# Attention scores from a stacked key and a 64-row product of the query's low part

## The chip, the cores and the metric

The kernel runs on one core of a Trainium2 chip. The metric is the device time of one execution in microseconds (us): less is better. TensorE (PE in the profile) multiplies matrices, VectorE (DVE), ScalarE (ACT) and GpSimd (POOL) work elementwise, and SyncE's queue (SP) issues the transfers. A matrix product on TensorE is two records: the load of the stationary operand (LDWEIGHTS, engine PEld) and the product proper (MATMUL, engine PE), through which the moving operand streams.

## The reference, cut to what matters

Two small networks follow each other on 512 tokens of width 1024, four layers in all. All arithmetic is float32. Three of the attentions have heads of width 64 and are touched here:

```python
# layer 2 of the first network: stick-breaking attention, 16 heads
z = jnp.einsum("bhqd,bhkd->bhqk", qb, k32) * scale
log_1m = jnp.where(mask, jax.nn.log_sigmoid(-z), 0.0)
suffix = lax.cumsum(log_1m, axis=3, reverse=True) - log_1m
wts = jnp.where(mask, jnp.exp(jax.nn.log_sigmoid(z) + suffix), 0.0)
...
# first layer of the second network: a global and a windowed attention, 8 query heads each, 2 key heads
s = jnp.einsum('bqkgd,bskd->bkgqs', qblk, k) * scale          # softmax, then times v
s = jnp.einsum('bqkgd,bskd->bkgqs', qblk, kb) * scale + bias
...
# second layer of the second network: attention to a neighbourhood, 16 heads
s = jnp.einsum('bqhd,bikhd->bhqik', qblk, kblk) * scale + bias
```

## The kernel before, in words

Every layer works on all 512 tokens with features on the partitions. TensorE takes its operands in a rounded type (fp32r), so each float32 operand x is split into a high part h, the rounded x, and a low part l = x - h. `split` makes them: ScalarE casts h (L204), GpSimd or VectorE subtracts (L206). A projection is three products for each 128 rows of the contraction (`mm3`: wh·xh, wh·xl, wl·xh, L169 to L171), 512 columns wide. Weights come through a ring: SP's queue fetches 256 KB (L149), ScalarE casts the high part (L150), VectorE subtracts the low part (L151).

A head has 64 features, so one tile of 128 partitions holds a pair of heads: head 0 on partitions 0 to 63, head 1 on 64 to 127. A product can contract over 128 partitions, twice a head's width. The kernel before uses this by stacking: `stack_q` copies, by transfers within the core's memory (L550, L551), the high part of a head's query to partitions 0 to 63 and its low part to 64 to 127 of one tile; `stack_k` copies the key's high part to both halves of one tile and its low part to both halves of a second (L565, L566). A score block is then two products over 128 rows with the same stationary operand (qh over ql): with kh over kh, and with kl over kl. This makes qh·kh + ql·kh + qh·kl + ql·kl. A pair costs 4 transfers for its query and 8 for its key, all issued in order on SP's queue among the weight fetches.

Scores are made in four places, always for a head at a time: `sb_score` (L664, L665; 8 pairs; blocks of 128, 256, 384 and 512 columns, and after them a product of an identity with a mask in bfloat16, L669 or L671, which adds the mask to the diagonal), `gqa_score` (L1128, L1129; 4 pairs, 512 columns), `win_score` (L1199, L1200; 4 pairs, 256 and 384 columns) and `na_score` (L1454, L1455; 8 pairs, 192 and 256 columns). Query pairs number 24 in all, key pairs 18 (4 query pairs share a key pair in the second network's first layer). The order of the code is the order on each engine: a pair's projection and stacking are written ahead of the values of the pair before it, so that they lie under its products.

One line elsewhere matters to the prediction: `window_bias` has a single product over 32 partitions with 8 stationary columns, in full float32:

```python
nc.tensor.matmul(ps[0:8], rb[0:32], sel[0:32], start=True, stop=True)   # L1173
```

Of the kernel before, what the change touches and what calls it, by code (L numbers as in the profile page):

```python
# [9 lines left out]
F32 = mybir.dt.float32  # L10
# [55 lines left out]
class Net:  # L66
# [476 lines left out]
    def stack_q(self, q32):  # L543

        nc = self.nc
        h, l = self.split(q32, "p")
        out = []
        for s in (slice(0, 64), slice(64, 128)):
            t = self.R.get()
            nc.sync.dma_start(t[0:64].bitcast(F32), h[s].bitcast(F32))  # L550
            nc.sync.dma_start(t[64:128].bitcast(F32), l[s].bitcast(F32))  # L551
            out.append(t)
        self.R.put(h, l)
        return out

    def stack_k(self, k32):

        nc = self.nc
        h, l = self.split(k32, "p")
        out = []  # L560
        for s in (slice(0, 64), slice(64, 128)):
            pair = []
            for part in (h, l):
                t = self.R.get()
                nc.sync.dma_start(t[0:64].bitcast(F32), part[s].bitcast(F32))  # L565
                nc.sync.dma_start(t[64:128].bitcast(F32), part[s].bitcast(F32))  # L566
                pair.append(t)
            out.append(pair)
        self.R.put(h, l)
        return out  # L570

    def v_evac(self, ps, r, out):

# [82 lines left out]
    def sb_score(self, QK, A, parts):  # L656

        nc = self.nc
        Q, K = QK
        ps = self.P.get()  # L660
        for n, (hd, i, o) in enumerate(parts):
            w = 128 * (i + 1)
            lhs = Q[hd][:, 128 * i : 128 * i + 128]
            nc.tensor.matmul(ps[:, o : o + w], lhs, K[hd][0][:, 512 - w : 512], start=n == 0, stop=False)  # L664
            nc.tensor.matmul(ps[:, o : o + w], lhs, K[hd][1][:, 512 - w : 512], start=False, stop=False)  # L665
        if len(parts) == 2:
            step = parts[1][2]
            diag = ps[:, : 2 * step].rearrange("p (n k) -> p n k", k=step)[:, :, 0:128]
            nc.tensor.matmul(diag, self.identb, self.sbmask.rearrange("p (n k) -> p n k", k=128), start=False, stop=True)  # L669
        else:  # L670
            nc.tensor.matmul(ps[:, 0:128], self.identb, self.sbmask[:, 0:128], start=False, stop=True)  # L671
        n = parts[-1][2] + 128 * (parts[-1][1] + 1)
        bt, b = self.f(n)
        at, a = self.f(n)
        nc.scalar.activation(a, ps[:, :n], AF.Sigmoid, scale=-1.0)  # L675
        nc.scalar.activation(b, ps[:, :n], AF.Sigmoid)
        self.P.put(ps)
        it, wt = self.F.get(), self.F.get()
        for hd, i, o in parts:
            w = 128 * (i + 1)  # L680
            nc.gpsimd.memset(it[:, o : o + 1], 1.0)  # L681
            nc.vector.tensor_tensor_scan(it[:, o + 1 : o + w], a[:, o : o + w - 1], self.zeros[:, : w - 1], 1.0, op0=ALU.mult, op1=ALU.add)  # L682
            nc.vector.tensor_tensor(wt[:, o : o + w], b[:, o : o + w][:, ::-1], it[:, o : o + w][:, ::-1], op=ALU.mult)
        self.F.put(bt, at, it)
        return wt

    def sb_weights(self, QK):
        W = {}
        for hd in range(2):
            w = self.sb_score(QK, hd, [(hd, 0, 0), (hd, 2, 128)])  # L690
            W[hd, 0], W[hd, 2] = (w, 0), (w, 128)
            W[hd, 3] = (self.sb_score(QK, hd, [(hd, 3, 0)]), 0)
        w = self.sb_score(QK, 0, [(0, 1, 0), (1, 1, 256)])
        W[0, 1], W[1, 1] = (w, 0), (w, 256)
        return W

    def sb_values(self, W, V, between):
# [61 lines left out]
    def sb_mixer(self, st, gain_next):  # L759
        nc = self.nc  # L760
# [22 lines left out]
        def scores():  # L783
            k = K.popleft()
            W = self.sb_weights((Q[0], k))
            self.R.put(*Q.popleft(), *k[0], *k[1])
            return W

        def some_out(tiles, upto):
# [331 lines left out]
    def gqa_score(self, Q, K, r8, hd):  # L1121
        nc = self.nc
        sums = self.small(4)
        tiles, pieces = [], []
        for b in range(4):
            ps = self.P.get()
            lhs = Q[:, 128 * b : 128 * b + 128]
            nc.tensor.matmul(ps, lhs, K[0], start=True, stop=False)  # L1128
            nc.tensor.matmul(ps, lhs, K[1], start=False, stop=True)  # L1129
            m = self.small(1)  # L1130
            nc.vector.reduce_max(m, ps, axis=AX.X)
            sc = r8[:, 2 * b + hd : 2 * b + hd + 1]
            nc.vector.scalar_tensor_tensor(m, m, -1.0, sc, op0=ALU.mult, op1=ALU.mult)
            t, p = self.f()
            nc.scalar.activation(p, ps, AF.Exp, scale=sc, bias=m, accum_out=sums[:, b : b + 1])
            self.P.put(ps)
            tiles.append(t)
            pieces.append((b, p))
        self.normalise(pieces, sums)
        return tiles, [x for _, x in pieces]  # L1140
# [40 lines left out]

    WIN = ((0, 256), (0, 384), (128, 384), (256, 256))

    def win_score(self, Q, K, hd):

        nc = self.nc
        tt, t = self.f(384)
        row = self.t5[hd : hd + 1, :]
        nc.sync.dma_start(t, bass.AP(row.tensor, row.offset, [[1, 128], [1, 384]]))
        bt, bias = self.f(384)  # L1190
        nc.vector.tensor_tensor(bias, t[:, ::-1], self.band, op=ALU.add)
        self.F.put(tt)
        sums = self.small(4)
        m = self.small(4)
        tiles, xs = [], []
        for b, (k0, n) in enumerate(self.WIN):
            ps = self.P.get()
            lhs = Q[:, 128 * b : 128 * b + 128]
            nc.tensor.matmul(ps[:, :n], lhs, K[0][:, k0 : k0 + n], start=True, stop=False)  # L1199
            nc.tensor.matmul(ps[:, :n], lhs, K[1][:, k0 : k0 + n], start=False, stop=True)  # L1200
            st, x = self.f(n)
            o = 128 if b == 0 else 0
            nc.vector.tensor_tensor_reduce(x, ps[:, :n], bias[:, o : o + n], 1.0, NEG, ALU.add, ALU.max, m[:, b : b + 1])
            self.P.put(ps)
            tiles.append(st)
            xs.append(x)
        self.F.put(bt)
        sink = self.p("sink", hd)
        neg = self.small(4)
        nc.vector.tensor_scalar(neg, m, sink, -1.0, op0=ALU.max, op1=ALU.mult)  # L1210
        for b, x in enumerate(xs):
            nc.scalar.activation(x, x, AF.Exp, bias=neg[:, b : b + 1], accum_out=sums[:, b : b + 1])
        es = self.small(4)
        nc.scalar.activation(es, neg, AF.Exp, bias=sink)
        nc.vector.tensor_tensor(sums, sums, es, op=ALU.add)
        self.normalise(list(enumerate(xs)), sums)
        return tiles, xs
# [45 lines left out]
    def even_mixer(self, st, gain_next):  # L1263
# [87 lines left out]
        for kind, score, value in (("a", self.gqa_score, self.gqa_value), ("b", self.win_score, self.win_value)):  # L1351
            K = got.pop(("k" + kind, 0))
            v = [[t[:, 256 * (kind == "b") + 128 * n :][:, 0:128] for t in V] for n in range(2)]
            for i in range(4):
                if kind == "a":
                    Q, r8 = got.pop(("qa", i))
                    W = [score(Q[n], K[n], r8, n) for n in range(2)]
                else:
                    Q = got.pop(("qb", i))
                    W = [score(Q[n], K[n], i + 4 * n) for n in range(2)]  # L1360
                self.R.put(*Q)
                more, after = [], None
                if i < 3:
                    emit("q" + kind, i + 1)
                    if kind == "a":
                        more.append(lambda: settle("qa", i + 1))
                elif kind == "a":
                    self.R.put(*K[0], *K[1])
                    emit("kb", 0)
                    emit("qb", 0)  # L1370
                else:
                    self.R.put(*K[0], *K[1])
                    self.start_out(outs, ("we_o",), 12, YH[:10], YL[:10], 1)
                    after = last
                keep(self.pair_values(value, W, v, gate(("g" + kind, i), *more), after))
# [51 lines left out]
            o = (15 - c) * 8  # L1427
            nc.sync.dma_start(self.nabias[:, 8 * c : 8 * c + 8, :], rows[:, :, o : o + 256])

    def na_score(self, Q, K, hd):  # L1430
        nc = self.nc
        tt, t = self.f(256)
        nc.sync.dma_start(t, self.nabias[hd])
# [13 lines left out]
        for x, parts in (  # L1447
# [2 lines left out]
        ):  # L1450
            ps = self.P.get()
            for b, k0, w, bias, o in parts:
                lhs = Q[:, 128 * b : 128 * b + 128]
                nc.tensor.matmul(ps[:, o : o + w], lhs, K[0][:, k0 : k0 + w], start=True, stop=False)  # L1454
                nc.tensor.matmul(ps[:, o : o + w], lhs, K[1][:, k0 : k0 + w], start=False, stop=True)  # L1455
            for b, k0, w, bias, o in parts:
                nc.vector.tensor_tensor_reduce(x[:, o : o + w], ps[:, o : o + w], bias, 1.0, NEG, ALU.add, ALU.max, m[:, b : b + 1])
                pieces.append((b, x[:, o : o + w]))
# [43 lines left out]
    def odd_mixer(self, st):  # L1502
# [95 lines left out]

        for i in range(8):
            Q, K = got.pop(("qc", i)), got.pop(("kc", i))  # L1600
            W = [self.na_score(Q[n], K[n], 2 * i + n) for n in range(2)]
            self.R.put(*Q, *K[0], *K[1])
            if i == 3:
                emit("v", 1)
                self.R.put(*edge)
# [250 lines left out]
```

## Time and profile before

| | |
|---|---|
| time, median of 3 runs | 1895.92 us (1894.84 to 1897.69) |
| the profiled execution's own time | 1898.73 us |
| its span, first to last instruction | 1896.9 us |
| PE busy | 1857.8 us, 98% |
| DVE, ACT, POOL busy | 63%, 47%, 16% |
| transfers within the core's memory for stacking | 240 of 128 KB |

The span is the time from the first to the last instruction of the profiled execution; the 1.8 us around it are start and end. Busy shares are means over stages that differ. A MATMUL's recorded duration (0.39 us for 512 columns) is longer than the distance to the next one (0.23 us), since products are pipelined: what a product costs is read from start to start.

### The profile page before, as it was taken

To read this page: it belongs to the slowest core of one execution; us is meant where nothing else is said; L and a number is where in the kernel's file an instruction comes from. 1 tells how busy PE (TensorE), PEld (TensorE's weight loads), DVE (VectorE), ACT (ScalarE), POOL (GpSimd) and SP (SyncE) were. 2 spreads that over 40 slices of the span, in tenths; PEclk is the share of its full clock that TensorE was granted. 3 is DMA by queue.
4 is the path that set the end of the run, shared out by engine and by line. 5 is a ranking of instruction groups with operands and counts; after the bars stand their busy time and mean duration, and the time that the engine had idled before them with its cause. 6 is when DMAs were issued, how large, how long until landed. Compare 5 with 4: busy or idle time off the path is not lost. (4 is left out here: it accounts for less than half of the span.)

```text
span 1896.9 us, 25808 instructions
## 1 busy us (share of the span) xinstructions
PE 1857.8 (98%) x9003; PEld 1550.5 (82%) x9003; DVE 1203.0 (63%) x2181; ACT 888.8 (47%) x1717; POOL 301.5 (16%) x354
## 2 busy tenths in 40 slices
PE   9989999999999999999999999999999999999998
PEld 6778888888888888788888889888888888888877
DVE  8886555553345998655554345779897655766753
ACT  6774333333335665533333344456665444545542
POOL 2332000000001221200000131222212411322310
PEclk9999999999999999999999999999999999999999
DMA  5333333333335542333333334322443433545522
GB/s 158 109 97 111 95 97 98 96 98 95 97 100 156 141 127 78 101 97 98 96 99 106 108 109 134 92 70 62 114 113 95 127 100 101 145 141 143 140 88 73
DMA packets 124802, 204.04 MB, mean 108 GB/s; under 512 B 21208, under 2 KB 31192, under 8 KB 124672
## 3 DMA queue, kind: packets, MB, share of 16 engines
q1 hardware_dynamic: 124672, 202.39, 37.1%
q8 instruction: 71, 1.16, 0.3%
q14 instruction: 59, 0.48, 0.1%
HBM read 168.76 MB, written 4.40 MB: 91 GB/s over the span
## 5 line engine op out<-in xcount | busy, mean ns | idle before, releaser
L171 PE MATMUL p<-r,wl 128*128 128x512 f32 (+1 forms) x2216 | 854.7, 386 | 9.2 <-DVE wl L151 9.2
L169 PE MATMUL p<-r,wh 128*128 128x512 f32 (+1 forms) x2216 | 857.7, 387 | 2.9 <-ACT wh L150 2.8
L170 PE MATMUL p<-r,wh 128*128 128x512 f32 (+1 forms) x2216 | 852.9, 385 | 0.3 <-POOL r L206 0.3
L150 ACT CAST wh<-w 128x512 fp32r<-128x512 f32 x608 | 371.6, 616 | 642.6 <-PE p L170 481.5
L151 DVE TENSOR_TENSOR wl<-w,wh 128x512 fp32r<-128x512 f32 x608 | 438.4, 725 | 345.8 <-ACT wh L150 345.0
L171 PEld LDWEIGHTS p<-r,wl 128*128 128x128 f32 x2216 | 417.9, 189 | 94.6 <-DVE wl L151 12.0
L169 PEld LDWEIGHTS p<-r,wh 128*128 128x128 f32 x2216 | 418.2, 189 | 86.4 <-ACT wh L150 5.5
L170 PEld LDWEIGHTS p<-r,wh 128*128 128x128 f32 x2216 | 418.1, 189 | 81.4 <-POOL r L206 1.1
L206 POOL TENSOR_TENSOR r<-f,r 128x512 fp32r<-128x512 f32 x102 | 139.8, 1371 | 501.9 <-ACT r L204 501.3
L204 ACT CAST r<-f 128x512 fp32r<-128x512 f32 x146 | 90.6, 621 | 182.5 <-DVE f L531 65.3
L220 POOL TENSOR_TENSOR f<-f,f 128x512 f32<-128x512 f32 x40 | 55.7, 1399 | 477.3 <-ACT f L214 477.2
L505 DVE TENSOR_TENSOR f<-p,f 128x512 f32<-128x512 f32 x68 | 46.9, 690 | 83.3 <-PE p L171 82.4
L620 DVE TENSOR_TENSOR r<-p,r 128x512 fp32r<-128x512 f32 (+2 forms) x152 | 90.4, 638 | 3.8 <-ACT r L619 3.2
L619 ACT CAST r<-p 128x512 fp32r<-128x512 f32 (+2 forms) x152 | 77.2, 557 | 10.7 <-PE p L1151 5.4
L596 PE MATMUL p<-wh,r 128*128 128x512 f32 (+1 forms) x192 | 71.7, 374 | 0.8 <-DVE f L609 0.8
L598 PE MATMUL p<-wh,r 128*128 128x512 f32 (+1 forms) x192 | 71.3, 372 | 0.0
L597 PE MATMUL p<-wl,r 128*128 128x512 f32 (+1 forms) x192 | 71.3, 372 | 0.0
L529 DVE TENSOR_TENSOR f<-p,f 128x512 f32<-128x512 f32 x44 | 30.4, 691 | 63.6 <-PE p L171 63.6
L508 ACT ACTIVATE f<-f 128x512 f32<-128x512 f32 x68 | 43.0, 633 | 38.4 <-DVE f L505 38.4
L964 DVE TENSOR_SCALAR f<-f,s 128x256 f32<-128x256 f32 (+3 forms) x160 | 56.4, 416 | 1.1
L682 DVE TENSOR_TENSOR_SCAN f<-f,f 128x127 f32<-128x127 f32 (+3 forms) x64 | 53.1, 869 | 6.3 <-ACT f L675 6.3
L681 POOL MEMSET f<- 128x1 f32 x64 | 5.2, 100 | 314.1 <-DVE f L509 208.3
(212 smaller groups left out, 1848.3 us busy)
## 6 DMA issues: line engine op xcount, KB each, us to landing
w<-w_gu SPq DMA_DIRECT2D x176, 256.0 KB, 2.9
r<-r SPq DMA_DIRECT2D x240, 128.0 KB, 2.4
w<-w_d SPq DMA_DIRECT2D x80, 256.0 KB, 2.7
w<-wo_m SPq DMA_DIRECT2D x64, 256.0 KB, 2.9
w<-we_m SPq DMA_DIRECT2D x52, 256.0 KB, 2.9
w<-w_rg SPq DMA_DIRECT2D x32, 256.0 KB, 2.9
w<-w_sqk SPq DMA_DIRECT2D x32, 256.0 KB, 2.9
w<-we_o SPq DMA_DIRECT2D x24, 256.0 KB, 2.6
```

What stands on the lines that cost most here:

```text
L150: nc.scalar.copy(h[:, :n], w[:, :n])
L151: nc.vector.tensor_tensor(l[:, :n], w[:, :n], h[:, :n].bitcast(F32), op=ALU.subtract)
L169: mm(out, wh, xh, start=start, stop=False)
L170: mm(out, wh, xl, start=False, stop=False)
L171: mm(out, wl, xh, start=False, stop=stop)
L204: nc.scalar.copy(h, src)
L206: e.tensor_tensor(l, src, h.bitcast(F32), op=ALU.subtract)
L596: mm(o, xh, h[:, s], start=st, stop=False)
L597: mm(o, xh, l[:, s], start=False, stop=False)
L598: mm(o, xl, h[:, s], start=False, stop=sp)
L619: nc.scalar.copy(h[:, :n], ps[:, :n])
L620: nc.vector.tensor_tensor(l[:, :n], ps[:, :n], h[:, :n].bitcast(F32), op=ALU.subtract)
```

## The change

`stack_q` now returns three tiles: a tile for head 0 with the query's high part on both halves, the same for head 1, and the split's low part l itself, which keeps head 0 on partitions 0 to 63 and head 1 on 64 to 127. `stack_k` returns one tile for each head: its high part on the half where the head lies, its low part on the other half. The half that needs no shift is written by ScalarE from the float32 source (cast to the rounded type), the other half by one transfer. A score block is a 128-row product (qh over qh with kh over kl) and a 64-row product (ql with kh, on the head's own partitions). The term ql·kl is left out. In `sb_score` the block of 256 columns, which both heads shared in one PSUM tile, is now a tile of its own for each head.

```diff
@@ stack_q
         h, l = self.split(q32, "p")
-        for s in (slice(0, 64), slice(64, 128)):
-            t = self.R.get()
-            nc.sync.dma_start(t[0:64].bitcast(F32), h[s].bitcast(F32))
-            nc.sync.dma_start(t[64:128].bitcast(F32), l[s].bitcast(F32))
+        a, b = self.R.get(), self.R.get()
+        nc.scalar.copy(a[0:64], q32[0:64])
+        nc.scalar.copy(b[64:128], q32[64:128])
+        nc.sync.dma_start(a[64:128].bitcast(F32), h[0:64].bitcast(F32))
+        nc.sync.dma_start(b[0:64].bitcast(F32), h[64:128].bitcast(F32))
+        self.R.put(h)
+        return [a, b, l]
@@ stack_k
         h, l = self.split(k32, "p")
-        for s in (slice(0, 64), slice(64, 128)):
-            for part in (h, l):
-                t = self.R.get()
-                nc.sync.dma_start(t[0:64].bitcast(F32), part[s].bitcast(F32))
-                nc.sync.dma_start(t[64:128].bitcast(F32), part[s].bitcast(F32))
+        a, b = self.R.get(), self.R.get()
+        nc.scalar.copy(a[0:64], k32[0:64])
+        nc.scalar.copy(b[64:128], k32[64:128])
+        nc.sync.dma_start(a[64:128].bitcast(F32), l[0:64].bitcast(F32))
+        nc.sync.dma_start(b[0:64].bitcast(F32), l[64:128].bitcast(F32))
+        return [a, b]
+    def score(self, out, Q, K, hd, qs, ks, start, stop):
+        mm = self.nc.tensor.matmul
+        rows = slice(64 * hd, 64 * hd + 64)
+        mm(out, Q[hd][:, qs], K[hd][:, ks], start=start, stop=False)
+        mm(out, Q[2][rows, qs], K[hd][rows, ks], start=False, stop=stop)
@@ sb_score (gqa_score, win_score and na_score likewise)
-            nc.tensor.matmul(ps[:, o : o + w], lhs, K[hd][0][:, 512 - w : 512], start=n == 0, stop=False)
-            nc.tensor.matmul(ps[:, o : o + w], lhs, K[hd][1][:, 512 - w : 512], start=False, stop=False)
+            self.score(ps[:, o : o + w], Q, K, hd, slice(128 * i, 128 * i + 128), slice(512 - w, 512), n == 0, False)
@@ sb_weights
-        w = self.sb_score(QK, 0, [(0, 1, 0), (1, 1, 256)])
-        W[0, 1], W[1, 1] = (w, 0), (w, 256)
+        for hd in range(2):
+            W[hd, 1] = (self.sb_score(QK, hd, [(hd, 1, 0)]), 0)
```

On TensorE the first scores of `gqa_score`, before. The first name behind the arrow is the moving operand (the key), the second the stationary one (the query); the size is the output's.

```order
L171 MATMUL p4_119<-r27_161,r34_168 128x512
L1128 MATMUL p6_121<-r39_173,r4_138 128x512
L1129 MATMUL p6_121<-r52_186,r4_138 128x512
L1128 MATMUL p7_122<-r39_173,r4_138 128x512
L1129 MATMUL p7_122<-r52_186,r4_138 128x512
L1128 MATMUL p2_117<-r39_173,r4_138 128x512
L1129 MATMUL p2_117<-r52_186,r4_138 128x512
```

And of the change, the same place (L571 is the 128-row product, L572 the one over 64 rows):

```order
L171 MATMUL p4_119<-r53_187,r42_176 128x512
L571 MATMUL p6_121<-r27_161,r46_180 128x512
L572 MATMUL p6_121<-r27_161,r50_184 128x512
L571 MATMUL p3_118<-r27_161,r46_180 128x512
L572 MATMUL p3_118<-r27_161,r50_184 128x512
L571 MATMUL p2_117<-r27_161,r46_180 128x512
L572 MATMUL p2_117<-r27_161,r50_184 128x512
```

The count, the widths and the place of the products stay; before, the moving tile alternates and the stationary one stays, now it is the other way round, and every second product covers half of the rows.

On SP's queue the stacking of the first pair of `na_score` (w32 is the weight ring), before:

```order
L149 DMA w32_2_222<-wo_m 128x512
L565 DMA r55_189<-r21_155 64x512
L566 DMA r55_189<-r21_155 64x512
L565 DMA r40_174<-r27_161 64x512
L566 DMA r40_174<-r27_161 64x512
L565 DMA r57_191<-r21_155 64x512
L566 DMA r57_191<-r21_155 64x512
L565 DMA r18_152<-r27_161 64x512
L566 DMA r18_152<-r27_161 64x512
L550 DMA r58_192<-r15_149 64x512
L551 DMA r58_192<-r32_166 64x512
L550 DMA r17_151<-r15_149 64x512
```

And of the change, the same place:

```order
L149 DMA w32_2_222<-wo_m 128x512
L562 DMA r43_177<-r21_155 64x512
L563 DMA r27_161<-r21_155 64x512
L149 DMA w32_0_220<-wo_m 128x512
L149 DMA w32_1_221<-wo_m 128x512
L550 DMA r41_175<-r48_182 64x512
L551 DMA r23_157<-r48_182 64x512
L149 DMA w32_2_222<-wo_m 128x512
```

Twelve transfers of one pair have become four, and two weight fetches now stand between the key's and the query's.

On TensorE the end of a pair's scores in `sb_score`, before, where both heads share a tile (p5) and one mask product:

```order
L664 MATMUL p5_120<-r24_158,r1_135 128x256
L665 MATMUL p5_120<-r32_166,r1_135 128x256
L664 MATMUL p5_120<-r40_174,r5_139 128x256
L665 MATMUL p5_120<-r44_178,r5_139 128x256
L669 LDWEIGHTS identb_129
L669 MATMUL p5_120<-sbmask_130,identb_129 128x2x128
```

And of the change:

```order
L571 MATMUL p5_120<-r24_158,r1_135 128x256
L572 MATMUL p5_120<-r24_158,r12_146 128x256
L671 LDWEIGHTS identb_129
L671 MATMUL p5_120<-sbmask_130,identb_129 128x128
L571 MATMUL p0_115<-r32_166,r5_139 128x256
L572 MATMUL p0_115<-r32_166,r12_146 128x256
```

A second mask product, into p0, follows this piece: there is one mask product more for each of the 8 pairs, and of the 64-row products six a pair are now followed by a mask.

## Rows read from the trace of the kernel before

**Rows 1.** The page: the span, and TensorE's busy time, share and instructions.

```profile
span 1896.9 us, 25808 instructions
PE 1857.8 (98%) x9003; PEld 1550.5 (82%) x9003; DVE 1203.0 (63%) x2181; ACT 888.8 (47%) x1717; POOL 301.5 (16%) x354
```

**Rows 2.** Stretches with scores: us, PE, PEld, DVE, ACT, POOL busy (x), PEclk, DMA share, GB/s.

```profile
1260.00:1362.00 102.00, 98.20 (x504) 81.03 (x504) 93.41 (x200) 65.39 (x138) 24.05 (x17) 1.00 0.33 89
1614.00:1830.00 216.00, 210.30 (x1117) 179.72 (x1117) 151.17 (x377) 110.15 (x273) 57.44 (x79) 0.99 0.47 133
```

**Rows 3.** One line's instructions: ns min/median/max, first and last start us, forms.

```profile
L664 PE MATMUL p<-r,r x64: 220/376/477, 582.5 to 738.5; 128*128 128x128 f32 x16, 128*128 128x384 f32 x16, 128*128 128x512 f32 x16, 128*128 128x256 f32 x16
L1128 PE MATMUL p<-r,r x32: 387/389/473, 1263.0 to 1337.4; 128*128 128x512 f32 x32
L1199 PE MATMUL p<-r,r x32: 274/334/356, 1361.8 to 1422.2; 128*128 128x256 f32 x16, 128*128 128x384 f32 x16
L1454 PE MATMUL p<-r,r x64: 249/282/330, 1617.9 to 1802.0; 128*128 128x192 f32 x32, 128*128 128x256 f32 x32
```

**Rows 4.** The timeline in `gqa_score`: start us, us, engine, line, operation, operands, rows*columns, size.

```profile
1263.72 0.39 PE L1129 MATMUL p<-r,r 128*128 128x512 f32 x1
1263.72 0.19 PEld L1128 LDWEIGHTS p<-r,r 128*128 128x128 f32 x1
1263.95 0.40 PE L1128 MATMUL p<-r,r 128*128 128x512 f32 x1
```

**Rows 5.** The timeline around the two 32-row products of L1173, TensorE and one cast.

```profile
1143.94 0.39 PE L171 MATMUL p<-r,wl 128*128 128x512 f32 x1
1144.14 0.62 ACT L150 CAST wh<-w 128x512 fp32r<-128x512 f32 x1 [0.74 <-DVE wl L151]
1144.26 0.09 PEld L1173 LDWEIGHTS p<-f,s 32*8 32x8 f32 x2 [0.35 <-issue]
1144.26 1.02 PE L1173 MATMUL p<-f,s 32*8 32x512 f32 x2
1145.21 0.19 PEld L169 LDWEIGHTS p<-r,wh 128*128 128x128 f32 x1 [0.86 <-ACT wh L150]
1145.32 0.19 PEld L170 LDWEIGHTS p<-r,wh 128*128 128x128 f32 x1
...
1145.44 0.28 PE L170 MATMUL p<-r,wh 128*128 128x256 f32 x1
```

**Rows 6.** L1173's products by line, and its operand's transfer (ns, start us).

```profile
L1173 PE MATMUL p<-f,s x2: 587/590/592, 1144.3 to 1144.7; 32*8 32x512 f32 x2
L1170 SPq DMA_DIRECT2D f<-c_t x1: 333/333/333, 1059.7 to 1059.7; - x1
```

**Rows 7.** The timeline where full-array products change their type from fp32r to float32.

```profile
1194.00 0.39 PE L171 MATMUL p<-r,wl 128*128 128x512 f32 x1
1194.01 0.64 PEld L1079 LDWEIGHTS p<-pair,f 128*128 128x128 f32 x4
1194.23 0.50 PE L1079 MATMUL p<-pair,f 128*128 128x2 f32 x4
```

**Rows 8.** The timeline around a mask product in `sb_score`.

```profile
582.88 0.33 PE L665 MATMUL p<-r,r 128*128 128x384 f32 x1
583.05 0.10 PEld L669 LDWEIGHTS <-identb 128*128 128x128 bf16 x1 [0.16 <-issue]
583.05 0.28 PE L669 MATMUL p<-sbmask,identb 128*128 128x256 bf16 x1
...
583.18 0.19 PEld L665 LDWEIGHTS p<-r,r 128*128 128x128 f32 x1
```

**Rows 9.** What TensorE's products waited for: us in total, times, longest us.

```profile
PE p L171 <- DVE wl L151: 9.2, 6, 2.6
PE p L1128 <- DMA r<-r: 2.7, 2, 1.5
PE p L1454 <- DMA r<-r: 2.0, 2, 1.2
```

**Rows 10.** Stacking transfers by issue (us to landing), one line's issues, and a 64-partition copy on ScalarE.

```profile
r<-r SPq DMA_DIRECT2D x240, 128.0 KB, 2.4
L551 SPq DMA_DIRECT2D r<-r x48: 461/584/2138, 569.7 to 1798.8; - x48
L608 ACT COPY f<-p 64x512 f32<-64x512 f32 x48 | 27.9, 581 | 20.0 <-PE p L1162 8.6 <-PE p L726 5.9 <-PE p L1240 3.9
```

More of the change, by code (lines that the diff above doesn't have):

```diff
@@ L546, in stack_q @@
         h, l = self.split(q32, "p")
-        out = []
-        for s in (slice(0, 64), slice(64, 128)):
-            t = self.R.get()
-            nc.sync.dma_start(t[0:64].bitcast(F32), h[s].bitcast(F32))
-            nc.sync.dma_start(t[64:128].bitcast(F32), l[s].bitcast(F32))
-            out.append(t)
-        self.R.put(h, l)
-        return out
+        a, b = self.R.get(), self.R.get()
[5 more added lines that the diff above has]
+        return [a, b, l]
     def stack_k(self, k32):
@@ L559, in stack_k @@
         h, l = self.split(k32, "p")
-        out = []
-        for s in (slice(0, 64), slice(64, 128)):
-            pair = []
-            for part in (h, l):
-                t = self.R.get()
-                nc.sync.dma_start(t[0:64].bitcast(F32), part[s].bitcast(F32))
-                nc.sync.dma_start(t[64:128].bitcast(F32), part[s].bitcast(F32))
-                pair.append(t)
-            out.append(pair)
-        self.R.put(h, l)
-        return out
+        a, b = self.R.get(), self.R.get()
[3 more added lines that the diff above has]
+        nc.sync.dma_start(b[0:64].bitcast(F32), l[64:128].bitcast(F32))
+        self.R.put(h, l)
+        return [a, b]
[4 more added lines that the diff above has]
+        mm(out, Q[2][rows, qs], K[hd][rows, ks], start=False, stop=stop)
     def v_evac(self, ps, r, out):
@@ L662, in sb_score @@
             w = 128 * (i + 1)
-            lhs = Q[hd][:, 128 * i : 128 * i + 128]
-            nc.tensor.matmul(ps[:, o : o + w], lhs, K[hd][0][:, 512 - w : 512], start=n == 0, stop=False)
-            nc.tensor.matmul(ps[:, o : o + w], lhs, K[hd][1][:, 512 - w : 512], start=False, stop=False)
+            self.score(ps[:, o : o + w], Q, K, hd, slice(128 * i, 128 * i + 128), slice(512 - w, 512), n == 0, False)
         if len(parts) == 2:
@@ L785, in scores @@
             W = self.sb_weights((Q[0], k))
-            self.R.put(*Q.popleft(), *k[0], *k[1])
+            self.R.put(*Q.popleft(), *k)
             return W
@@ L1126, in gqa_score @@
             ps = self.P.get()
-            lhs = Q[:, 128 * b : 128 * b + 128]
-            nc.tensor.matmul(ps, lhs, K[0], start=True, stop=False)
-            nc.tensor.matmul(ps, lhs, K[1], start=False, stop=True)
+            self.score(ps, Q, K, hd, slice(128 * b, 128 * b + 128), slice(0, 512), True, True)
             m = self.small(1)
@@ L1182, with win_score @@
     WIN = ((0, 256), (0, 384), (128, 384), (256, 256))
-    def win_score(self, Q, K, hd):
+    def win_score(self, Q, K, hd, side):
         nc = self.nc
@@ L1197, in win_score @@
             ps = self.P.get()
-            lhs = Q[:, 128 * b : 128 * b + 128]
-            nc.tensor.matmul(ps[:, :n], lhs, K[0][:, k0 : k0 + n], start=True, stop=False)
-            nc.tensor.matmul(ps[:, :n], lhs, K[1][:, k0 : k0 + n], start=False, stop=True)
+            self.score(ps[:, :n], Q, K, side, slice(128 * b, 128 * b + 128), slice(k0, k0 + n), True, True)
             st, x = self.f(n)
@@ L1356, in even_mixer @@
                     Q, r8 = got.pop(("qa", i))
-                    W = [score(Q[n], K[n], r8, n) for n in range(2)]
+                    W = [score(Q, K, r8, n) for n in range(2)]
                 else:
                     Q = got.pop(("qb", i))
-                    W = [score(Q[n], K[n], i + 4 * n) for n in range(2)]
+                    W = [score(Q, K, i + 4 * n, n) for n in range(2)]
                 self.R.put(*Q)
@@ L1367, in even_mixer @@
                 elif kind == "a":
-                    self.R.put(*K[0], *K[1])
+                    self.R.put(*K)
                     emit("kb", 0)
@@ L1371, in even_mixer @@
                 else:
-                    self.R.put(*K[0], *K[1])
+                    self.R.put(*K)
                     self.start_out(outs, ("we_o",), 12, YH[:10], YL[:10], 1)
@@ L1428, in grid_bias, with na_score @@
             nc.sync.dma_start(self.nabias[:, 8 * c : 8 * c + 8, :], rows[:, :, o : o + 256])
-    def na_score(self, Q, K, hd):
+    def na_score(self, Q, K, hd, side):
         nc = self.nc
@@ L1452, in na_score @@
             for b, k0, w, bias, o in parts:
-                lhs = Q[:, 128 * b : 128 * b + 128]
-                nc.tensor.matmul(ps[:, o : o + w], lhs, K[0][:, k0 : k0 + w], start=True, stop=False)
-                nc.tensor.matmul(ps[:, o : o + w], lhs, K[1][:, k0 : k0 + w], start=False, stop=True)
+                self.score(ps[:, o : o + w], Q, K, side, slice(128 * b, 128 * b + 128), slice(k0, k0 + w), True, True)
             for b, k0, w, bias, o in parts:
@@ L1600, in odd_mixer @@
             Q, K = got.pop(("qc", i)), got.pop(("kc", i))
-            W = [self.na_score(Q[n], K[n], 2 * i + n) for n in range(2)]
-            self.R.put(*Q, *K[0], *K[1])
+            W = [self.na_score(Q, K, 2 * i + n, n) for n in range(2)]
+            self.R.put(*Q, *K)
             if i == 3:
```

## The prediction

> **What bounds the kernel now.** I read the page first: TensorE is busy for 1857.8 of 1896.9 us, and no other engine for more than 63% [rows 1]. So the time is TensorE's instruction stream plus few gaps, and a change counts by what it does to that stream. The stretches with scores say the same: in 1260 to 1362 us TensorE is busy for 98.20 of 102 us, in 1614 to 1830 us for 210.30 of 216 us, at a granted clock of 1.00 and 0.99, its upper level [rows 2]. VectorE comes close in the first of them (93.41 us) but TensorE still waits little for it. Then the timeline of a score block: products of 512 columns start 0.23 us apart, and the next product's load starts in the same instant as the product ahead of it [rows 4]. Loads are thus hidden; a score block costs its columns and nothing else. Last, the waits: products waited for stacking transfers four times, 4.7 us in all [rows 9].
>
> **What goes.** 156 of 240 transfers [rows 10]: 24 query pairs lose 2 each, 18 key pairs lose 6. They lie on SP's queue and the transfer engines, both off the path, except where a score waits. There the first score now waits for two transfers of the query's high part (not for the low part's too) and, in the last stage, for a queue shorter by 8 issues of some 0.58 us, so I take the whole 4.7 us as gone. The bound below is 0 (the waits move to another operand), above some 10 us (part of the 9.2 us for late weights too, which share the queue [rows 9]).
>
> **What is added beside other work.** ScalarE gets 84 casts of 64 partitions by 512; the nearest row, a 64x512 copy, takes 581 ns [rows 10], so 49 us on an engine with 47% busy [rows 1], two behind each split. They lie under the projections that follow, where the weight ring stands ahead; uncovered, two casts would delay the next weight by 1.2 us a stacking, 42 times, 49 us. I take 0: even in the densest stretch ScalarE is busy for 65.39 of 102 us [rows 2]. The stick-breaking attention also has 8 mask products more. A 256-wide mask takes 0.13 us, from 583.05 to the next load at 583.18 [rows 8]; one of 128 columns about half, and two instead of one cost some 0.06 us more a pair: 0.5 us. The split of the two 512-wide sigmoids of a pair into four lies on ScalarE: nothing.
>
> **What changes on the path: the shape of every second score product.** Count and columns stay. There are 64 + 32 + 32 + 64 = 192 blocks [rows 3], so 192 products become 64 rows high, each between two of 128 rows: 384 changes of shape. What does one cost? The trace has no 64-row product, but it has one place with another shape, the two 32-row products of L1173. Ahead of them stands an ordinary 512-column product at 1143.94; the next should stream at 1144.17, and its load should have begun beside the product. Instead the load begins at 1144.26, 0.09 us late [rows 5]. Its data was there: the operand's transfer was issued at 1059.7 [rows 6]. On the way back the second product starts at 1144.26 + 1.02 - 0.59 = 1144.69 and, like the first, lasts 0.43, to 1145.12; the load of the next 128-row product begins only at 1145.21, again 0.09 late, and the load after it follows at 1145.32, so that 0.11 us of loading lie open too [rows 5]. The wait that the profile names there, a cast, had ended at 1144.76. The change of type is not the cause: where full-array products go from fp32r to float32, the load starts at 1194.01 beside the product of 1194.00 and the next product follows 0.23 us after it [rows 7]. So a change of shape costs 0.09 us until the load may begin and 0.11 us of open load: 0.20 us.
>
> The Trainium skill speaks against the change in the same sense: "TensorEngine Tiling (Array Packing)", section Key Properties, says that changing the tiling mode, not just the tile, drains the engine, and its list of modes has a 64-row one; with an open drain only, the sum would be that of the half-price rival below. The trace agrees at its one place.
>
> The lower bound of this price is 0 (the row has 8 columns and 32 rows; either may be what counts), the upper 0.20 us. I take 0.20, since this row is the only one with fewer rows, and both of its directions agree.
>
> **The sum.** 144 blocks have 256 columns or more [rows 3]: 288 changes by 0.20 us are 57.6. At 192 columns the stream needs 0.09 us (0.23 by 192/512) but the hidden load already sets 0.11, so the excess is 0.18: 64 changes, 11.5 us. At 128 columns it is 0.06 against 0.11, excess 0.15: 32 changes, 4.8 us. Six of eight 64-row products of a stick-breaking pair are followed by a mask, whose load leaves no visible gap (the 384-wide product ahead of it needs 0.17 us and the mask starts 0.17 after it [rows 8]): 48 changes save the 0.11 of open load, less 4.8 us with what the mask's load takes itself. Together 69.1 us. Masks add 0.5, the transfers give back 4.7, and about 1 us comes back where TensorE waits for VectorE today (it has more time to catch up in 1260 to 1440 us). That is +63.9 us on the profiled execution's own 1898.7 us: 1962.6. This execution lay 2.8 us above the median of 1895.9, so against the median the forecast is 1960 us.
>
> **The rivals.** *The 64-row shape costs nothing* (ends faster): if its load may run beside a 128-row product, only the transfers count: 1895.9 - 4.7 + 0.5 = 1891.7, from 1886 to 1896. It is decided by the price of a change: below 4.2/384 = 0.011 us the change gains. For it: 32 rows by 8 columns differ in columns too, and every 128-row load is hidden [rows 4]. Against it: the only row of fewer rows. The Trainium skill has a rule for this side, "TensorE: Matmul & The Clock Gate", section Step-by-step: what each phase is for: a load is pulled ahead of running products when it goes to the background buffer; the loads of 128 rows here do so, the 32-row one did not.
>
> *Half the price*: the engine drains for 0.09 us and the load is hidden, or the load of 0.11 us is open without a drain. 384 by 0.09 is 34.6; 0.11 open for the wide blocks, less for the narrow ones and not ahead of masks, is some 35 as well. Less 5: about 1926 us (1915 to 1938).
>
> *ScalarE becomes late on top of the full price*: two casts sit ahead of the next weight's cast in ScalarE's order, and TensorE waits for the low part of that weight. Up to 49 us more: 1980 to 2010. Against it: 47% busy.
>
> **Chances.** Full price 0.52 (1945 to 1975), half 0.16, more 0.07, nothing 0.25. A measurement of this kernel tells about 0.2%, 3.8 us, from no change; of the last case 0.15 lie below 1892.1 and 0.10 above. So faster 0.15, same 0.10, slower 0.75. The range must take in the free case and ends above the full price: 1888 to 1977 us.
>
> **What would show it.** Right: in each score block the 64-row loads no longer start beside the product ahead but some 0.09 us after its stream's end, and products of 512 columns start 0.43 us apart instead of 0.23; score stretches grow by about 3 us a pair in the global attention (16 changes) and nothing grows in projections; the waits for stacking transfers in [rows 9] are gone. Wrong: 64-row loads beside the product ahead, as in [rows 4], and starts 0.23 us apart; or new waits of weights for ScalarE; or a fall of the granted clock in the score stretches.

## The result

| | before | after |
|---|---|---|
| median | 1896.81 us (1894.84 to 1898.55, 4 runs) | 1974.49 us (1971.09 to 1976.36, 4 runs) |
| profiled execution, its span | 1898.73, 1896.9 us | 1976.36, 1974.6 us |
| mean granted clock of TensorE | 0.993 | 0.977 |

After over before is 1.0405 (95% interval 1.0392 to 1.0418): slower, by 77.7 us where +64 was forecast. The price of a change of shape came out as forecast. Two other terms did not: TensorE's clock fell in and behind the score stretches, and more waits than thought came back.

### The profile page after: what moved, and what is told of

It is laid out like the page before. It is cut to its first block, busy times and chain, and to the rows that moved or that the text cites. A ratio compares the mean times of both kernels' runs of the same rounds, so it can differ in the third digit from the quotient of the medians.

```text
span 1974.6 us, 25634 instructions
## 1 busy us (share of the span) xinstructions
PE 1948.3 (99%) x9011; PEld 1584.8 (80%) x9011; DVE 1194.1 (60%) x2181; ACT 946.4 (48%) x1817; POOL 301.5 (15%) x354
## 4 chain that ended last, share of the span: by engine, by line
PE 58%; DVE 1%; issue 1%; POOL 0%; ACT 0%; POOLq 0%; DVEq 0%
PE p L169 15%; PE p L171 15%; PE p L170 15%; PE p L572 2%; PE p L571 2%; PE p L598 1%; PE p L600 1%; PE p L599 1%; PE p L1469 1%; PE p L1149 1%; PE p L1487 0%; PE p L1486 0%; PE p L1225 0%; PE p L1000 0%; PE p L1160 0%
## 5 line engine op out<-in xcount | busy, mean ns | idle before, releaser
L169 PE MATMUL p<-r,wh 128*128 128x512 f32 (+1 forms) x2216 | 868.0, 392 | 2.1 <-ACT wh L150 2.1
L170 PE MATMUL p<-r,wh 128*128 128x512 f32 (+1 forms) x2216 | 861.0, 389 | 0.9 <-DVE r L229 0.6
L151 DVE TENSOR_TENSOR wl<-w,wh 128x512 fp32r<-128x512 f32 x608 | 433.1, 715 | 350.5 <-ACT wh L150 349.2
L171 PEld LDWEIGHTS p<-r,wl 128*128 128x128 f32 x2216 | 422.5, 191 | 96.3 <-DVE wl L151 11.4
L169 PEld LDWEIGHTS p<-r,wh 128*128 128x128 f32 x2216 | 422.8, 191 | 90.2 <-ACT wh L150 5.0
L170 PEld LDWEIGHTS p<-r,wh 128*128 128x128 f32 x2216 | 422.9, 191 | 83.4 <-DVE r L229 1.3
L572 PE MATMUL p<-r,r 64*128 64x192 f32 (+4 forms) x192 | 83.3, 434 | 0.0
L571 PE MATMUL p<-r,r 128*128 128x192 f32 (+4 forms) x192 | 78.8, 410 | 0.0
L572 PEld LDWEIGHTS p<-r,r 64*128 64x128 f32 x192 | 37.1, 193 | 34.9 <-issue 24.4
L682 DVE TENSOR_TENSOR_SCAN f<-f,f 128x127 f32<-128x127 f32 (+3 forms) x64 | 49.0, 806 | 15.1 <-ACT f L675 15.1
```

What stands on the lines that cost most here:

```text
L151: nc.vector.tensor_tensor(l[:, :n], w[:, :n], h[:, :n].bitcast(F32), op=ALU.subtract)
L169: mm(out, wh, xh, start=start, stop=False)
L170: mm(out, wh, xl, start=False, stop=False)
L171: mm(out, wl, xh, start=False, stop=stop)
L571: mm(out, Q[hd][:, qs], K[hd][:, ks], start=start, stop=False)
L572: mm(out, Q[2][rows, qs], K[hd][rows, ks], start=False, stop=stop)
```

## The profile after

The page of after, span, engines and TensorE's granted clock in 40 slices, against [rows 1]:

```profile
span 1974.6 us, 25634 instructions
PE 1948.3 (99%) x9011; PEld 1584.8 (80%) x9011; DVE 1194.1 (60%) x2181; ACT 946.4 (48%) x1817; POOL 301.5 (15%) x354
PEclk9999999999999999999999999989889999999899
```

TensorE has 8 products more (the masks) and is busy for 90.5 us longer; every other engine's share is about what it was. That share alone would call TensorE fuller, not slower. The timeline of a global-attention score shows what it is full of (start us, us, engine, line, operation, rows*columns, size, idle time before it). It answers to [rows 4]:

```profile
1282.45 0.18 PEld L572 LDWEIGHTS p<-r,r 64*128 64x128 f32 x1 [0.31 <-issue]
1282.45 0.49 PE L572 MATMUL p<-r,r 64*128 64x512 f32 x1
1282.87 0.19 PEld L571 LDWEIGHTS p<-r,r 128*128 128x128 f32 x1 [0.24 <-issue]
1282.87 0.50 PE L571 MATMUL p<-r,r 128*128 128x512 f32 x1
1283.30 0.18 PEld L572 LDWEIGHTS p<-r,r 64*128 64x128 f32 x1 [0.24 <-issue]
1283.31 0.50 PE L572 MATMUL p<-r,r 64*128 64x512 f32 x1
```

Products of 512 columns start 0.43 us apart where they started 0.23 apart. No load lies beside the product ahead of it any more: load and product share a start. The product's recorded 0.50 us holds the open load; the 0.24 us of idle loader before it, "issue", is the time in which the next load could have run and did not. It is the same in both directions, 128 to 64 rows and back.

The second thing is seen in the windows of one such stretch (length, busy us of PE, PEld, DVE, ACT, POOL with counts, granted clock, DMA share, GB/s):

```profile
1268.00:1282.00 14.00, 14.00 (x72) 11.76 (x71) 10.70 (x23) 8.71 (x20) 4.79 (x4) 1.00 0.23 72
1282.00:1285.70 3.70, 3.70 (x11) 1.62 (x9) 3.64 (x9) 1.39 (x3) 1.42 (x2) 1.00 0.43 144
1285.70:1295.90 10.20, 10.20 (x19) 5.80 (x19) 5.76 (x16) 4.89 (x12) 0.57 (x1) 0.50 0.01 2
1295.90:1305.00 9.10, 9.10 (x49) 7.72 (x48) 6.62 (x15) 5.10 (x10) 0.80 (x1) 1.00 0.17 58
```

And in the timeline inside the third window:

```profile
1288.16 0.79 PE L571 MATMUL p<-r,r 128*128 128x512 f32 x1
1288.89 0.79 PE L572 MATMUL p<-r,r 64*128 64x512 f32 x1
1289.61 0.79 PE L571 MATMUL p<-r,r 128*128 128x512 f32 x1
...
1292.50 0.63 PE L169 MATMUL p<-r,wh 128*128 128x512 f32 x1
1292.93 0.63 PE L170 MATMUL p<-r,wh 128*128 128x512 f32 x1
```

From 1282.13 TensorE alternates between the two shapes; at 1285.70 the granted clock falls from its upper level (2.4 GHz) to its lower one (1.2 GHz). Score products then start 0.72 us apart, and the ordinary projection products behind them 0.43 apart instead of 0.23, until 1295.90. TensorE is busy for 100% of each of these stretches by the profile. Over the whole execution the mean clock of 0.977 means 2 x 0.023 x 1974.6 = 91 us at the lower level; before, with 0.993, it was 27 us.

What TensorE did ahead of a fall differs. The same view for the 3 us ahead of a fall, in the kernel before and then in the change:

```profile
1810.60:1813.60 3.00, 1.62 (x11) 1.20 (x12) 2.31 (x10) 3.00 (x12) 0.00 (x0) 1.00 0.00 0
1419.20:1422.20 3.00, 3.00 (x11) 1.58 (x9) 2.60 (x8) 0.58 (x1) 0.00 (x0) 1.00 0.38 133
```

In the kernel before, TensorE stood idle for part of the 3 us ahead of each of its six falls. In the change this is so for 5 of 18; ahead of the other 13 it was busy throughout, and 6 to 9 changes of shape lie in the 3 us.

The waits of TensorE's products, all those above 1 us (us in total, times, longest), against [rows 9]:

```profile
PE p L171 <- DVE wl L151: 8.4, 6, 2.6
PE p L169 <- ACT wh L150: 2.1, 2, 1.1
PE p L1111 <- DVE f L1107: 1.8, 1, 1.8
PE p L1651 <- POOL s L239: 1.5, 2, 1.0
PE p L115 <- DVE s L359: 1.2, 1, 1.2
PE p L252 <- POOL k L239: 1.2, 1, 1.2
```

The waits for stacking transfers are gone. All rows of this view sum to 19.3 us; before they summed to 31.8.

## Experiments

The theory: each change of row count costs a drain and an open load. Its rivals were that something else in the change is dear (the casts, the operand tiles, the split block, the transfers), or that a 64-row product is slow by itself. Each kernel was timed beside the kernel before on its chip; ratios are to that.

**e1, no 64-row product.** The query's low part gets a tile for each head, filled with zeros on the other half; POOL does two fills and two half subtractions for a pair.

```diff
-        mm(out, Q[2][rows, qs], K[hd][rows, ks], start=False, stop=stop)
+        mm(out, Q[2 + hd][:, qs], K[hd][:, ks], start=False, stop=stop)
```

> The change, but the product of the query's low part runs over 128 rows: each head gets its own low tile, with zeros on the other head's 64 partitions (two fills and two subtractions on GpSimd for a pair instead of one subtraction). Transfers, casts, columns and stationary operands stay as in the change. If the change of row count is the cost: back to 1890 to 1898 us, 512-column score products 0.23 us apart, granted clock as before (0.99). If the casts on ScalarE, the new stacking or the alternating stationary operand cost: still 1940 us or more.

1914.32 us, ratio 1.0078 (1.0061 to 1.0095), clock 0.991: between the two ranges of the expectation. Some 60 of the 78 us go with the 64-row shape. What is left, 15 us, is for the greater part in waits: TensorE's products wait 41.8 us in all, 10 more than before, most of all for weights of the stick-breaking attention and for operands of the global one's values (e5 and e11 take up the first). In the profiled executions, which lie 17 us apart, most of the rest goes with the clock (0.991 against 0.993).

```profile
PE p L715 <- DVE f L685: 10.5, 6, 2.0
...
PE p L1162 <- DVE r L624: 5.7, 6, 1.8
```

**e2, the kernel before with 64-row products only.** The second product of each block covers rows 0 to 63 alone; it leaves out ql·kl. Tiles, transfers and casts are those of before.

```diff
-            nc.tensor.matmul(ps, lhs, K[1], start=False, stop=True)
+            nc.tensor.matmul(ps, lhs[0:64], K[1][0:64], start=False, stop=True)
```

> The kernel before, with all its 240 transfers and no new cast; only the second score product is cut to 64 rows (the query's high part with the key's low part; the product of the two low parts is left out, as in the change). If the row count is the cost: 1960 to 1985 us, the whole loss of the change in one edit. If the loss comes from casts, stacking or the alternating stationary operand: 1890 to 1900 us.

1980.87 us, ratio 1.0432 (1.0417 to 1.0448), clock 0.976. One edit brings the whole loss, the fall of the clock with it:

```profile
1283.84 0.18 PEld L1129 LDWEIGHTS p<-r,r 64*128 64x128 f32 x1 [0.25 <-issue]
1283.84 0.50 PE L1129 MATMUL p<-r,r 64*128 64x512 f32 x1
1284.27 0.19 PEld L1128 LDWEIGHTS p<-r,r 128*128 128x128 f32 x1 [0.24 <-issue]
1284.27 0.50 PE L1128 MATMUL p<-r,r 128*128 128x512 f32 x1
```

**e3 and e4, the same products in another order.** e3 turns the order of the two products round in every second block, so that two of a shape follow each other. e4 makes all 128-row products of a head, then all its 64-row ones. The work is that of the change. The scheduler of the framework moves some products, so the changes of row count are counted in the traces: 384 in the change, 246 in e3, 114 in e4.

```diff
+        if self.turn:
+            two.reverse()
+        self.turn = not self.turn
```

> The change, but the order of the two products alternates from block to block (128, 64, 64, 128, ...): the same 192 products of 64 rows, but 240 changes of row count instead of 384. If the price is paid at a change of row count: the loss shrinks to 55 to 65% of the change's, 1937 to 1950 us. If it is paid by each 64-row product: 1970 to 1978 us as the change.

> The change, but within a head all 128-row products (and masks) come first and then all 64-row ones: 96 changes of row count instead of 384, the same products. If the price is paid at a change: 1905 to 1920 us (96 by 0.2 us, less the transfers' 5 us, and little loss of clock). If each 64-row product pays: 1970 us or more. If holding up to four PSUM tiles makes TensorE wait for VectorE and ScalarE, new waits show at the first product of the head after.

e3: 1932.55 us, 1.0178 (1.0163 to 1.0193), clock 0.988. This is below its range: 42% of the change's loss is left where 55 to 65% was expected, since part of the clock came back with the changes. e4: 1907.64 us, 1.0048 (1.0032 to 1.0064), clock 0.993, in its range. Four products of each shape in e4's global attention:

```profile
1271.72 1.08 PE L571 MATMUL p<-r,r 128*128 128x512 f32 x4
1272.73 0.76 PEld L572 LDWEIGHTS p<-r,r 64*128 64x128 f32 x4 [0.36 <-POOL s L239]
1272.73 1.19 PE L572 MATMUL p<-r,r 64*128 64x512 f32 x4
1273.85 0.76 PEld L571 LDWEIGHTS p<-r,r 128*128 128x128 f32 x4 [0.36 <-ACT r L204]
```

From 1272.73 to 1273.85 four 64-row products take 1.12 us: four streams of 0.23 and one change of 0.20. A 64-row product by itself is thus no dearer than one of 128 rows, and its load hides beside another of its shape. The parts of the 0.20 us are seen in the single records, the last 128-row product and the first two loads of 64 rows:

```profile
1272.41 0.39 PE L571 MATMUL p<-r,r 128*128 128x512 f32 x1
1272.73 0.18 PEld L572 LDWEIGHTS p<-r,r 64*128 64x128 f32 x1 [0.36 <-POOL s L239]
1272.84 0.19 PEld L572 LDWEIGHTS p<-r,r 64*128 64x128 f32 x1
```

The product's stream ends at 1272.64, 0.23 us after its start; the first load begins 0.09 us after that, and the load behind it 0.11 us later.

The time goes with the changes: 42 us for the first 138 that fall away (0.30 each), 25 us for the next 132 (0.19 each), with the clock's return in both (0.977, 0.988, 0.993).

**e5, no 64-row product and no work for POOL.** The key's high part also goes to tiles whose other half stays zero; the low product runs over 128 rows with them, at two more casts a key pair.

```diff
-        mm(out, Q[2][rows, qs], K[hd][rows, ks], start=False, stop=stop)
+        mm(out, Q[2][:, qs], K[2 + hd][:, ks], start=False, stop=stop)
```

> The change with no 64-row product: the low part of the query keeps its tile for both heads as a 128-row stationary operand, and each head gets a second key tile with its high part on its own half and zeros on the other, written once in tiles that are kept for the purpose; two casts more on ScalarE for a key pair, no work more on GpSimd. If row changes are the whole loss and the 15 us of the padded low part (e1) came from GpSimd's fills and second subtraction: 1888 to 1897 us, with the change's four transfers a pair. If 128-row products with an alternating stationary operand cost anything themselves, or the casts do: 1905 us or more.

1909.07 us, ratio 1.0052 (1.0039 to 1.0066): in the second range of the expectation, not the first. Neither 64-row shapes, POOL work nor most transfers are left, and it is still 9 us slower than before. Its waits name the place:

```profile
PE p L726 <- DVE f L696: 9.3, 6, 2.4
```

These are the transposes of the stick-breaking weights, waiting for VectorE's last multiplication but one of a pair. The same wait in the kernel before:

```profile
PE p L713 <- DVE f L683: 0.3, 1, 0.3
```

VectorE gets the sigmoids late. ScalarE's timeline behind the query's split, e5 and then the kernel before (one pair, the same place):

```profile
642.05 0.62 ACT L204 CAST r<-f 128x512 fp32r<-128x512 f32 x1 [1.12 <-DVE f L656]
642.58 0.61 ACT L548 CAST r<-f 64x512 fp32r<-64x512 f32 x1
643.22 0.62 ACT L549 CAST r<-f 64x512 fp32r<-64x512 f32 x1
643.86 0.60 ACT L688 ACTIVATE f<-p 128x512 f32<-128x512 f32 x1
```

```profile
640.57 0.62 ACT L204 CAST r<-f 128x512 fp32r<-128x512 f32 x1 [0.33 <-DVE f L641]
641.10 0.59 ACT L675 ACTIVATE f<-p 128x512 f32<-128x512 f32 x1
```

From split to first sigmoid is 0.53 us before and 1.81 us with the two casts: 1.28 us more in a pair. The split itself is late too. Its input is VectorE's eviction of the query's projection, which starts 0.20 us after the pair's first score before, but 2.2 us after it in three of the six pairs behind the first in e5 and 0.6 in two. So the first sigmoid comes 4.8 and 3.1 us after the first score there, against 1.45 before.

**e11, the casts alone.** The kernel before, with the change's 84 casts into a tile that nothing reads.

```diff
         h, l = self.split(q32, "p")
+        t = self.R.get()
+        nc.scalar.copy(t[0:64], q32[0:64])
+        nc.scalar.copy(t[64:128], q32[64:128])
+        self.R.put(t)
```

> The kernel before plus the change's 84 casts of 64 partitions on ScalarE, two behind each split, into a tile that nothing reads; all else as before. If the casts alone delay the sigmoids of the stick-breaking attention by 1.3 us a pair, over 0.5 us of room: some 0.8 us of wait at the transposes in six pairs, and up to as much again in the global and windowed attention: 1900 to 1907 us. If ScalarE's spare time hides them, as the prediction took it: within 2 us of before.

1905.33 us, ratio 1.0040 (1.0027 to 1.0053), 7.9 us over before, and the same wait:

```profile
PE p L721 <- DVE f L691: 7.7, 6, 1.4
```

So the casts cost some 8 us where nothing covers them, with what they set off: in e11 the eviction comes 1.0 us after the first score from the third pair on. In the change this wait doesn't appear. There the scores of a pair take longer: by the timeline a pair's first transpose starts 13.61 us after its first score in five of seven pairs and 15.1 us in the other two, instead of 11.19, and the last multiplication has ended after 12.4 us. TensorE comes later than the late operand.

**e7 and e8, what else delays e5.** e7 puts the query's casts behind the sigmoids; e8 gives the 256-column blocks of both heads one tile again, as before.

```diff
+                for f in later:
+                    f()
```

> As e5 (128-row products only), with one order changed: in the stick-breaking attention the query's two casts are issued after the scores of the pair ahead instead of before them. If these casts make the sigmoids late and TensorE's transposes wait for them (11 us of waits within the values in e5): 1897 to 1901 us. If not: within 2 us of e5, 1907 to 1911.

> As e5, with the block of 256 columns of both heads in one PSUM tile again, as before the change (two sigmoids of 512 instead of four of 256, one mask instead of two). If the split of this tile is what makes the transposes wait: 1897 to 1901 us. If the casts are: within 3 us of e5.

e7: 1906.60 us, 1.0043 (1.0029 to 1.0056), not the gain hoped for. e8: 1906.99 us, 1.0055 (1.0042 to 1.0068). The split of the block is not the cause, and deferring the casts is not enough. In e7 the sigmoids of a pair no longer stand behind casts, but the eviction of the query's projection comes 2.2 us after the pair's first score in four of these six pairs, much as in e5. It stands behind subtractions for weights on VectorE. That these weights arrive earlier on the emptier queue doesn't explain it alone: the change has the same queue, and its eviction starts after 0.20 us. How e5's 9 us divide between casts and this order wasn't separated further.

**e6, e9, two heads in turn.** e6 is e4, but in the stick-breaking and the neighbourhood attention the 64-row products of two heads alternate; they stand on opposite halves of the rows. e9 does so everywhere and defers the casts. Counted changes: 112 and 114.

```diff
+        half = len(low) // 2
+        for f in [f for two in zip(low[:half], low[half:]) for f in two]:
+            f()
```

> As e4 (96 changes of row count), but in the stick-breaking and the neighbourhood attention the 64-row products of the two heads follow each other in turn, one on partitions 0 to 63, the next on 64 to 127; again 96 changes of row count. If only the row count of a product matters: within 3 us of e4. If a change of the half also costs 0.2 us: 18 us or more above e4 (some 90 changes of half more). If products on different halves run side by side: up to 8 us below e4, with starts of 64-row products much less than 0.11 us apart.

> e6 with the casts issued late as in e7, and the 64-row products of the two heads also in turn in the global and the windowed attention, two blocks of each head at a time. If 64-row products on different halves run side by side everywhere and the casts no longer delay: 1886 to 1896 us, faster than before. If the pairs of heads make TensorE wait for VectorE instead: 1897 us or more.

e6: 1900.36 us, 1.0011 (1.0002 to 1.0020). e9: 1898.93 us, 1.0004 (0.9996 to 1.0013). e6 lies 7 us below e4 at the same number of changes (6 us where both run at a clock of 0.996). Eight 64-row products of e6's neighbourhood attention (four of 192 columns, four of 256), which the view puts into one row with the size of the first:

```profile
1784.18 0.52 PEld L572 LDWEIGHTS p<-r,r 64*128 64x128 f32 x8
1784.18 0.72 PE L572 MATMUL p<-r,r 64*128 64x192 f32 x8
1784.83 0.19 PEld L169 LDWEIGHTS p<-r,wh 128*128 128x128 f32 x1
```

1792 columns would stream for 0.79 us at 0.227 us for 512; here the next load begins 0.65 us after the first product, with a change of 0.20 in it: 0.45 us of streaming. Products on opposite halves run side by side.

**e10, 64 rows throughout.** No stacking, no transfers, no casts beyond the split's: three 64-row products (qh·kh, ql·kh, qh·kl) for a block, two heads in turn. 92 changes.

```diff
+            lambda: mm(out, qh, kh, start=start, stop=False),
+            lambda: mm(out, ql, kh, start=False, stop=False),
+            lambda: mm(out, qh, kl, start=False, stop=stop),
```

> No stacking at all: no transfer and no cast beyond the split. Each score block is three 64-row products (high by high, low by high, high by low part), those of the two heads in turn on the two halves of the array, in groups of two tiles of each head or of one; masks after a group. If products on different halves run side by side everywhere, a pair of blocks costs three streams of columns instead of four, some 14 us less of TensorE's time, against some 100 row changes by 0.18 us, 18 us, and the waits for transfers, casts and late weights of the earlier versions go: 1885 to 1896 us. If only part of them overlap, or the groups make TensorE wait for VectorE: 1898 us or more.

1897.18 us, ratio 0.9998 (0.9989 to 1.0007). In its timeline one row stands for the products of both heads:

```profile
640.08 0.40 PE L558 MATMUL p<-r,r 64*128 64x512 f32 x2
640.32 0.39 PE L559 MATMUL p<-r,r 64*128 64x512 f32 x2
```

Two products of 512 columns take 0.24 us together, as long as one. All 240 transfers are gone and the time is that of before. New waits stand where those for transfers stood:

```profile
PE p L169 <- ACT f L1152: 5.6, 4, 1.7
PE p L1179 <- DVE r L621: 2.3, 3, 0.9
PE p L169 <- DVE s L1223: 2.1, 2, 1.0
```

The gain that was hoped for from e9 (1886 to 1896 us) and e10 (1885 to 1896) did not come: no version beats the kernel before by more than can be measured.

## Why the prediction was right, and where its sum was off

To divide the 77.7 us I took, in both traces, the distance from each product's start to the next one's and subtracted what its columns need (0.227 us for 512, at least 0.112), then sorted the rest by whether one of the two products has 64 rows and by the clock's level.

| term | forecast, us | in the trace, us |
|---|---|---|
| changes of shape, clock at its upper level | 69.1 for all 384 | 61.9 for 349 |
| the other 35, clock at its lower level | | 13.9 |
| other products, clock at its lower level | 0 | +22.5 |
| columns and masks | +0.5 | +0.8 |
| waits given back | -5.7 | -21.5 |
| sum | +63.9 | +77.6 |

*The price of a change* was the step on which all hung, and it held: 0.180 us on average in the forecast, 61.9/349 = 0.177 measured. A place with two 32-row products [rows 5] was enough to price 64-row ones: 512-column products lie 0.43 us apart, as written, and the split into 0.09 us of drain and 0.11 us of open load is seen in e4. Between its first and last score product a pair of the global attention took 3.5 us before where nothing waited and 6.3 to 6.6 us in the change, the 3 us that were written (8.2 where the clock fell in it). The average hides errors that nearly cancel: ahead of a mask the open load is not saved (47 such changes at the upper level cost 0.20 us each, 9.4 us, where the sum has 4.8), and changes at narrow blocks cost less (0.08 or 0.14 us at 128 columns, 0.15 to 0.17 at 192, where the sum has 0.15 and 0.18). The Trainium skill says in "TensorEngine Tiling (Array Packing)", Key Properties, that a switch of mode drains the engine. The traces agree, with 0.09 us until the load begins; the open load behind it doubles the price.

*Free* and *half price* fell at once with the timeline; e2 and e4 show that it is the change and not the shape that costs.

*The clock* is the step that failed. The forecast named a fall of the granted clock as what would make it wrong, and gave it no price. It also wrote that nothing would grow in projections; those behind a fall did, from 0.23 to 0.43 us a product. At the lower level are 91 us instead of 27. That is 22.5 us on products of unchanged shape, and 13.9 - 35 x 0.18 = 7.6 us on the changes themselves: 30 us. That it comes from the alternation is shown by the change (0.977) against e4 (0.993), the same products in another order, and by e2 (0.976), which alternates without the rest of the change. Falls without idle time ahead of them are in the traces of the change, e2 and e3, and in no other. Why the clock falls at one place in a stretch and not at another the runs don't tell.

*The waits given back* were undersized: 21.5 us instead of 5.7. Transfers are 4.7 of it [rows 9], as forecast. Another 7.8 us were waits for VectorE and others behind scores, which are seen in the waits (31.8 less 19.3, less 4.7). I had put 1 us there. An engine that gets 70 us more time catches up with more than its longest waits. The last 9 us are mostly no gaps but sorting: pairs with a score product or a mask had 4.3 us beyond their columns before, which stood in this row of the division; nearly all of these pairs now count as changes, and those that don't make -2.7 us. These 7 us belong to the changes, which thus added some 0.16 us each to the time before. The two errors, +30 and -16, make up the difference of 14.

That the time stayed within the stated range, and 0.5 us below the upper end of the full-price case (1975), is partly luck: with the clock's 30 us alone the forecast of 1960 would have become 1990.

*The casts at nothing* was right for the change, but for a reason that the prediction did not give. I argued from ScalarE's 47% busy time and the weight ring. e11 shows 8 us when they stand uncovered, and not at the weights but in front of the sigmoids, which have some 0.7 us of room (from e11's third pair on they come 2.05 us later, and the second transpose of a pair 1.4). What covered them was TensorE's own slowing. So the rival "ScalarE late on top" was wrong for this kernel, and "cost nothing" would not have come out at 1892 either, had the shape been free: e5 is near that case (with two more casts a key pair), and it is 1.0052 of before.

*The transfers*: e10 has none and waits as long in all as the kernel before (31.2 and 31.8 us), now on ScalarE and VectorE. Since e10 changes the products and their order too, what the transfers alone are worth is not shown.

Not tried: hiding the drain or the load alone behind other work.

## What to carry to other kernels

Before halving the rows of a product to save operands, count how often the row count would change along TensorE's order: each change costs about 0.2 us here at 256 columns or more, so group products of one shape, or run two half-height products on opposite halves together. An edit that is free under a slower engine must be priced again without it, at the place where its engine has least room, not by its busy share. When the spacing of TensorE's products widens, read the granted clock of the stretch and of the products behind it, even at a busy share of 99%.

## What the runs showed of the hardware

Alternating between 128 and 64 rows brings the granted clock down to its lower level in places, while TensorE is busy for 100% of the stretch by the profile, since the records of its products meet across drain and open load. Seen in the change, e2 and, less, e3 (0.977, 0.976, 0.988), not in the grouped orders (0.993 to 0.996) and not before, where each fall comes behind idle time.

64-row products on opposite halves of the rows run side by side: two of 512 columns in 0.24 us (e10). The Trainium skill says this of tiles on distinct row groups in "TensorE: Matmul & The Clock Gate", Part 3; e6 and e10 agree for tiles of 64 rows.

A cast of 64 partitions by 512 takes ScalarE 0.62 us, as long as one of 128 partitions (e5's timeline). Half the partitions save nothing there.
